# Sixteen weight splits made ahead move from the dilated heads to the convolution

## The chip, the cores and the metric

One core of a Trainium2 chip runs the whole program. The metric is the device time of one execution in microseconds: the median of several runs.

## The reference

Two transformer blocks run behind one another on one sequence of 1024 positions and 1024 channels, in float32. The first block has two layers, a gated short convolution and a dilated attention with 8 heads; the second an attention over selected keys and a gated feed-forward with a convolution. Cut to what matters here:

```python
mod = silu(c) @ w_mod + b_mod                      # per layer: shift, scale, gate
h, gate = rms_norm(x, g) * (1 + scale) + shift, gate
# layer 0
b_gate, c_gate, xin, z = split(h @ conv_w_in, 4)
x = x + gate * ((b_gate * conv3(c_gate * xin) * silu(z)) @ conv_w_out)
# layer 1: per head 3 groups (rates 1, 4, 16) of q and k, one v, one z
q, k, v, z = split(h @ dil_w_in, ...)              # q, k rotated
o = softmax-weighted sum over the groups of banded_attention(q_g, k_g, v)
x = x + gate * ((o * silu(z)) @ dil_w_out)
# second block: a_w_in, a_w_qi, a_w_uq, a_w_uk, a_w_uv, a_w_o, then f_w_in, f_w_out
```

## The kernel before

**Products.** A float32 product is made of three TensorE matmuls, high times high, high times low and low times high; every operand is kept as a rounded part `hi` and a rest `lo`. All of them are recorded at line 256. `gemm` multiplies one weight of 128 by 1024 with both halves of 512 positions: 24 matmuls for each half.

**Weights.** There are two ways to get one. `weight()` loads the raw weight on SyncE's queue (L376) into one of three slots `wraw`, ScalarE copies its high part (L377) and GpSimd subtracts (L378) into one of three pairs `wring`. `ready()` does this ahead, for the weights of the second block (`w2i` to `w3i`, 64 steps): a load (L353) into a slot of the same ring `wraw`, a copy by ScalarE into the one page `bench` (L354), a subtraction by VectorE in place (L355), and two stores to memory of the chip, of the high part (L357) and of the low part (L358). Later `weight()` loads such a pair in one go. Each step is started by `later.go()`. A slot of `wraw` is free again when the subtraction (L378), or the second store (L358), has read it.

**Order.** SyncE issues all these loads and stores in one queue, in a fixed order: an L357 waits for ScalarE, an L358 for VectorE, and an L353 or L376 for its slot, and what stands behind waits too. Each engine works in a fixed order as well. A scheduler sets these orders at build time; it simulates the engines and moves instructions of independent work past one another, so the order is not that of the code.

**The convolution** (L648 to L661) runs over columns j of 128 channels. A column has four weights `w0i` (`conv_cx`, `conv_zb`), whose products go to banks of PSUM in turn. VectorE reads them, at L561 (c times x) and L572 (b times z), and so frees the banks; `conv_out` makes the convolution and the gate. Beside it `modvec` makes the vectors of later layers: each `modblock` loads 512 KB of `wmod` (L298) into a page in turn, VectorE multiplies and sums it (L301) and adds the bias (L303). Some `w1v` weights of the next layer are loaded there too (L699). SyncE's names for the pages of `wmod` are `page_829` to `page_831`.

**The heads** (L945 to L981). For each of 8 heads six blocks of q and k are made, three groups of each, a block z, and then `attend`, whose scores go to PSUM (128x256 products) and are taken out by VectorE: L771 takes the maximum of two rows of blocks of the first group, in two pairs of instructions, one for each bank; L775 follows; L790 does it for the other groups. Between them L978 makes the gate from z, in two halves. In the code before, a split ahead is started after each of the six blocks, after z, and after `attend`: 8 in a head, 64 in all.

The function is long; the program prints here what the change touches.

Of the kernel before, what the change touches and what calls it, by code (L numbers as in the profile page):

```python
# [200 lines left out]
def emit(tc, I, OUT):  # L201
# [14 lines left out]
    with sp as sp, pp as pp, dp as dp:  # L216
# [34 lines left out]
        ar = Arena(pages, page_tile)  # L251
# [135 lines left out]
        def gemm(w, h, chunks, m=128, tag="mm"):  # L387

            whi, wlo = w
            out = {c: psum(tag) for c in chunks}  # L390
            kn = whi.shape[1]
            for c in chunks:
                for k in range(kn):
                    hi, lo = h[k][c]
                    mm(out[c][:m], whi[:, k], hi.r, k == 0, False)
                    mm(out[c][:m], whi[:, k], lo.r, False, False)
                    mm(out[c][:m], wlo[:, k], hi.r, False, k == kn - 1)
            return out
# [76 lines left out]
        def free_h(H, c):  # L475
            for k in range(len(H)):
                for b in H[k][c]:
                    b.free()
                H[k][c] = None
# [84 lines left out]
        def conv_zb(j, chunks, sz, ws=None, pz=None, pb=None):  # L564
            wz, wb = ws or (weight(I["w0i"][24 + j]), None)
            pz = pz or gemm(wz, H, chunks)
            for c in chunks:
                sz[c] = ar.new(512)
                A.activation(sz[c].f, pz[c], AF.Silu)
            pb = pb or gemm(wb or weight(I["w0i"][j]), H, chunks, tag="po")  # L570
            for c in chunks:
                V.tensor_mul(sz[c].f, sz[c].f, pb[c])  # L572

        def conv_out(j, t, sz):
            for c in range(2):
                u = ar.new(512)
                tv = lambda d: t.f[:, 512 * c + d:512 * c + d + 512]
                kc = lambda d: ck[d][:, j:j + 1]
                A.activation(u.f, tv(1), AF.Copy, scale=kc(1))
                V.scalar_tensor_tensor(u.f, tv(0), kc(0), u.f, op0=OP.mult, op1=OP.add)  # L580
                V.scalar_tensor_tensor(u.f, tv(2), kc(2), u.f, op0=OP.mult, op1=OP.add)
                V.tensor_mul(u.f, u.f, sz[c].f)
                Y[j][c] = new2()
                split(*Y[j][c], u.f, engine=G)
                u.free()
                sz[c].free()
            t.free()
# [56 lines left out]
            b.free()  # L644
        mring.extend(ar.new(1024) for _ in range(3))
        conv_out(0, *ts[0])
        pending = [2, 3, 4, 5, 6, 7, 8, 9, 10, 11]
        for j in range(1, 8):  # L648
            t, sz = ts[1] if j == 1 else new_t()
            if j > 1:  # L650
                conv_cx(j, (0, 1), t)
                conv_zb(j, (0, 1), sz)
            if j == 7:
                free_h(H, 0)
                free_h(H, 1)
            conv_out(j, t, sz)
            for _ in range(2 if j in (1, 3, 5) else 1):
                modvec(pending.pop(0))

        def weight_own(src, bufs):  # L660
# [4 lines left out]
            raw.free()  # L665
            bufs.extend((hi, lo))
            return tuple(b.r.rearrange("p (k m) -> p k m", k=8) for b in (hi, lo))

        bench = []
        later = Steps(ready(["w2i", "w2k", "w2q", "w2uk", "w2uv", "w2uq", "w2o", "w3i"]))  # L670

        def outproj(win, Y, c, gate, xold, xnew, each, apart=()):

# [271 lines left out]
        for h in range(HEADS):  # L945
# [5 lines left out]
            for g in range(3):  # L951
                for t, off, pad in ((q, 0, 0), (k, 24, 64)):
                    p = block(off + 8 * g + h)
                    later.go()
                    for c in range(2):
                        if g == 0:
                            at = lambda v: v[:, pad + 512 * c:pad + 512 * c + 512]
                        else:
                            at = lambda v: v.rearrange("p (j n) -> p n j",
                                                       j=8)[:, 64 * c:64 * c + 64]  # L960
# [7 lines left out]
                for b, part in zip(vs[-1], vd):  # L968
                    dma(b.f.rearrange("p (t n) -> p t n", n=128), src(part))
            p = block(56 + h)  # L970
            later.go()
            if h == HEADS - 1:
                free_h(H, 0)
                free_h(H, 1)
# [3 lines left out]
                V.scalar_tensor_tensor(sz.f[:, CH(c)], sz.f[:, CH(c)], 1.0, p[c], op0=OP.add,  # L978
                                       op1=OP.mult)
            attend(h, q, k, vs, sz)  # L980
            later.go()  # L981
        later.finish()
        for b in rope + mask1:
            b.free()
# [686 lines left out]
```

## Time and profile before

| | |
|---|---|
| median of 3 runs | 2758.61 us (2758.21 to 2761.03) |
| the profiled execution | 2767.96 us, span 2766.2 us, mean granted clock 0.974 |
| TensorE (PE) busy | 2610.6 us, 94% |
| VectorE (DVE) busy | 1535.2 us, 55% |
| ScalarE (ACT) busy | 1123.5 us, 41% |
| GpSimd (POOL) busy | 1001.8 us, 36% |
| L355, the splits' subtraction | 64 of them, 85.9 us |
| L354, the splits' copy | 64 of them, 67.4 us |

The convolution ends near 416 us, the heads run from about 600 to 1400 us, the second block from there to the end. TensorE's share is high in all stages, so an engine's busy time tells little; the idle time of TensorE, the wait that ends it, and the granted clock, which is 1.0 at 2.4 GHz, tell where time lies. Idle time of another engine matters only where TensorE stands behind it.

### The profile page before, as it was taken

What the parts mean: (1) busy time and instruction counts of PE and PEld (TensorE: products, weight loads), DVE (VectorE), ACT (ScalarE), POOL (GpSimd) and SP (SyncE); (2) the same over time, 40 slices, a digit from 0 to 9 for tenths busy, and PEclk for the clock granted to TensorE, in tenths of its full rate; (3) what the DMA queues carried; (4) which work ended last, traced back from release to release, by engine and by line L of the source; (5) the groups of instructions that cost most, each with busy time, mean ns of one, the idle gap of its engine ahead of it and who ended that gap; (6) DMA issues with size and microseconds to landing.
All of it is one profiled execution on the core that took longest, in us unless ns stands there. A gap on an engine that the chain in (4) does not pass through costs nothing. (4 is left out here: it accounts for less than half of the span.)

```text
span 2766.2 us, 34054 instructions
## 1 busy us (share of the span) xinstructions
PE 2610.6 (94%) x12070; PEld 2150.3 (78%) x12070; DVE 1535.2 (55%) x3260; ACT 1123.5 (41%) x1938; POOL 1001.8 (36%) x770
## 2 busy tenths in 40 slices
PE   8998999899999999999989888899999989999998
PEld 7886888788877878878867666678788767878887
DVE  7697222324666666666676699899655540222211
ACT  4211223324545545545443657674444432111132
POOL 1132327415535535535546334212211165200053
PEclk9999999999999999999999989999999999999999
DMA  7476214566365465456445573686666763667632
GB/s 291 162 273 234 88 66 158 163 202 220 131 229 198 140 220 206 141 203 214 157 140 177 205 247 103 229 262 224 207 212 213 242 203 103 207 239 259 226 117 73
DMA packets 208582, 524.67 MB, mean 190 GB/s; under 512 B 22258, under 2 KB 82202, under 8 KB 192796
## 3 DMA queue, kind: packets, MB, share of 16 engines
q1 hardware_dynamic: 199052, 497.20, 52.4%
q0 software_dynamic: 9216, 25.17, 3.1%
q8 instruction: 95, 1.56, 0.2%
q14 instruction: 75, 0.61, 0.1%
q10 hardware_dynamic: 144, 0.14, 0.0%
HBM read 394.03 MB, written 129.97 MB: 189 GB/s over the span
## 5 line engine op out<-in xcount | busy, mean ns | idle before, releaser
L256 PE MATMUL p<-page,wring 128*128 128x512 f32 (+2 forms) x8586 | 2023.9, 393 | 62.7 <-ACT page L384 11.4
L256 PEld LDWEIGHTS p<-page,wring 128*128 128x128 f32 (+1 forms) x8586 | 1605.9, 190 | 411.4 <-issue 20.2
L256 PE MATMUL p<-page,page 128*128 128x512 f32 (+5 forms) x2811 | 592.4, 354 | 75.3 <-DVE page L771 11.6
L378 POOL TENSOR_TENSOR wring<-wraw,wring 128x1024 fp32r<-128x1024 f32 (+1 forms) x159 | 392.6, 2471 | 599.2 <-ACT wring L377 532.5
L256 PEld LDWEIGHTS p<-page,page 128*128 128x128 f32 (+1 forms) x2811 | 470.5, 201 | 165.5 <-issue 18.1
L377 ACT ACTIVATE wring<-wraw 128x1024 fp32r<-128x1024 f32 (+1 forms) x159 | 164.4, 1035 | 317.6 <-PE p L256 285.2
L385 POOL TENSOR_TENSOR page<-page,page 128x512 fp32r<-128x512 f32 (+1 forms) x87 | 132.2, 1528 | 397.4 <-ACT page L384 390.9
L384 ACT ACTIVATE page<-page 128x512 fp32r<-128x512 f32 (+1 forms) x136 | 87.1, 652 | 227.5 <-DMA page<-d 104.1
L735 POOL TENSOR_TENSOR page<-page,page 128x512 f32<-128x512 f32 x96 | 123.8, 1296 | 87.8 <-ACT page L734 87.8
L355 DVE TENSOR_TENSOR wraw<-wraw,page 128x1024 fp32r<-128x1024 f32 (+1 forms) x64 | 85.9, 1342 | 92.1 <-ACT page L354 82.5
L301 DVE SCALAR_TENSOR_TENSOR page<-page,page 128x1024 f32<-128x1024 f32 x88 | 116.4, 1323 | 34.3 <-DMA page<-wmod 34.1
L1543 DVE SCALAR_TENSOR_TENSOR page<-p,page,page 128x512 f32<-128x512 f32 (+1 forms) x17 | 12.2, 719 | 204.1 <-PE p L256 204.1
L354 ACT ACTIVATE page<-wraw 128x1024 fp32r<-128x1024 f32 (+1 forms) x64 | 67.4, 1054 | 142.3 <-DMA wraw<-w3i 73.4
L744 POOL TENSOR_TENSOR page<-page,page 128x512 fp32r<-128x512 f32 x64 | 95.7, 1496 | 60.3 <-ACT page L743 60.2
L742 DVE TENSOR_TENSOR page<-page 128x512 f32<-128x512 f32 x64 | 98.0, 1532 | 27.8 <-POOL page L735 27.8
L737 DVE TENSOR_TENSOR page<-p,page 128x512 f32<-128x512 f32 x96 | 66.0, 687 | 66.4 <-ACT page L734 62.0
L1267 ACT ACTIVATE page<-page,page 128x1024 bf16<-128x1024 f32 (+1 forms) x93 | 86.7, 933 | 35.4 <-DVE page L1290 31.1
L743 ACT ACTIVATE page<-page 128x512 fp32r<-128x512 f32 x64 | 57.1, 892 | 84.5 <-DVE page L742 84.2
L1377 POOL TENSOR_TENSOR page<-page,page 128x256 f32<-128x256 f32 x64 | 46.7, 737 | 107.5 <-DVE page L1397 51.5
L441 POOL TENSOR_TENSOR page<-page,page 128x512 f32<-128x512 f32 x39 | 52.2, 1338 | 85.2 <-ACT page L440 85.1
L683 DVE SCALAR_TENSOR_TENSOR page<-p,page,page 128x512 f32<-128x512 f32 x48 | 35.9, 748 | 84.2 <-PE p L256 84.1
L1270 DVE TENSOR_SCALAR_CACHE_REDUCE page<-page,page 128x768 bf16<-128x768 f32 (+1 forms) x93 | 81.5, 876 | 1.5
(214 smaller groups left out, 2303.4 us busy)
## 6 DMA issues: line engine op xcount, KB each, us to landing
wring<-d SPq DMA_DIRECT2D x122, 1024.0 KB, 5.8
d<-page SPq DMA_DIRECT2D x95, 512.0 KB, 3.8
page<-wmod SPq DMA_DIRECT2D x88, 512.0 KB, 4.5
d<-page SPq DMA_DIRECT2D x153, 256.0 KB, 4.0
d<-wraw SPq DMA_DIRECT2D x63, 512.0 KB, 3.5
page<-d SPq DMA_DIRECT2D x121, 256.0 KB, 3.2
wraw<-w1i SPq DMA_DIRECT2D x56, 512.0 KB, 3.5
wraw<-w3i SPq DMA_DIRECT2D x44, 512.0 KB, 3.3
```

The costliest lines, as they stand in the source:

```text
L256: lastn["mm"] = T.matmul(out, lhsT=l, rhs=r, start=start, stop=stop)
L301: V.scalar_tensor_tensor(w.f, w.f, 1.0, sil[j // 6].f, op0=OP.mult, op1=OP.mult, accum_out=m)
L355: V.tensor_sub(raw.r[:, :n], raw.f[:, :n], hi.f[:, :n])
L377: A.activation(hi.r[:, :n], raw.f[:, :n], AF.Copy)
L378: (lo_engine or G).tensor_sub(lo.r[:, :n], raw.f[:, :n], hi.f[:, :n])
L384: A.activation(hi.r[:, :n], src, AF.Copy)
L385: (engine or V).tensor_sub(lo.r[:, :n], src, hi.f[:, :n])
L735: G.tensor_mul(sw.f, sw.f, rope[1].f[:, CH(c)])
L742: V.tensor_tensor(a.f, a.f, sw.f, op=OP.add)
L744: G.tensor_sub(out[1], shape(a.f), out[2])
L1267: A.activation(junk.b[:, 0:sc.n], sc.f, AF.Sign, scale=-1.0, bias=at, accum_out=one)
L1270: V.tensor_scalar(junk.b[:, 0:sc.n], sc.f, at, None, op0=OP.is_ge, op1=OP.add, accum_out=one)
```

## The change

The two calls of `later.go()` after z and after `attend` are taken out of the head, so a head starts six splits and the eight heads 48. The generator and `bench` are made before the convolution. For columns 4 to 7 `later.go(4)` starts four splits in each, between `conv_zb` and `conv_out`, with a page for `bench` that is taken at column 4 and given back at column 7. The 64 steps keep their order, so in the convolution the 16 are `w2i` (4), `w2k`, `w2q`, `w2uk`, `w2uv`, `w2uq` (2 each of the last three) and four of `w2o`. Lines after 659 have moved by 3 and after 970 by 2 or 1 (L771 is now L774, L775 L778, L790 L793, L978 L980).

```diff
@@ -644,13 +644,19 @@
         conv_out(0, *ts[0])
+        bench = []
+        later = Steps(ready(["w2i", "w2k", "w2q", "w2uk", "w2uv", "w2uq", "w2o", "w3i"]))
         pending = [2, 3, 4, 5, 6, 7, 8, 9, 10, 11]
         for j in range(1, 8):
             t, sz = ts[1] if j == 1 else new_t()
             if j > 1:
                 conv_cx(j, (0, 1), t)
                 conv_zb(j, (0, 1), sz)
+            if j == 4:
+                bench.append(ar.new(1024))
+            later.go(4 if j > 3 else 0)
             if j == 7:
+                bench.pop().free()
                 free_h(H, 0)
                 free_h(H, 1)
             conv_out(j, t, sz)
...
-        bench = []
-        later = Steps(ready(["w2i", "w2k", "w2q", "w2uk", "w2uv", "w2uq", "w2o", "w3i"]))
...
             p = block(56 + h)
-            later.go()
...
             attend(h, q, k, vs, sz)
-            later.go()
         later.finish()
```

How this moves instructions is seen at three places. The first is SyncE's queue in the convolution, from the last raw weight of column 4 on. Before:

```order
L376 DMA wraw<-w0i 128x1024
L699 DMA page_831<-w1v 128x1024
L298 DMA page_829<-wmod 128x1024
L298 DMA page_830<-wmod 128x1024
L298 DMA page_829<-wmod 128x1024
L298 DMA page_830<-wmod 128x1024
L376 DMA wraw<-w0i 128x1024
L298 DMA page_829<-wmod 128x1024
L298 DMA page_830<-wmod 128x1024
```

and in the changed kernel:

```order
L376 DMA wraw<-w0i 128x1024
L298 DMA page_829<-wmod 128x1024
L298 DMA page_830<-wmod 128x1024
L298 DMA page_829<-wmod 128x1024
L298 DMA page_830<-wmod 128x1024
L298 DMA page_829<-wmod 128x1024
L353 DMA wraw<-w2i 128x1024
L298 DMA page_830<-wmod 128x1024
L298 DMA page_829<-wmod 128x1024
L357 DMA d_1677<-page_1130 128x1024
L358 DMA d_1677<-wraw 128x1024
L298 DMA page_830<-wmod 128x1024
```

The `w1v` load has moved behind, and between the `wmod` loads stand the load and the two stores of the first split; the next raw `w0i` comes at row 126 of the queue instead of 111.

The second place is VectorE at the products of column 4 (L561, which empties two banks), among the products of `wmod` (L301). Before:

```order
L561 TENSOR_TENSOR page_440<-page_832,p_1510 128x512
L301 SCALAR_TENSOR_TENSOR page_830,page_65<-page_830,page_88 128x1024
L580 SCALAR_TENSOR_TENSOR page_1130<-page_440,page_65,page_1130 128x512
L303 TENSOR_TENSOR page_65<-page_65 128x1
L591 MEMSET page_440 128x1
L301 SCALAR_TENSOR_TENSOR page_829,page_65<-page_829,page_88 128x1024
L303 TENSOR_TENSOR page_65<-page_65 128x1
L301 SCALAR_TENSOR_TENSOR page_830,page_65<-page_830,page_88 128x1024
L561 TENSOR_TENSOR page_440<-page_84,p_1511 128x512
```

and in the changed kernel:

```order
L355 TENSOR_TENSOR wraw<-wraw,page_1130 128x1024
L301 SCALAR_TENSOR_TENSOR page_830,page_65<-page_830,page_88 128x1024
L301 SCALAR_TENSOR_TENSOR page_829,page_65<-page_829,page_88 128x1024
L303 TENSOR_TENSOR page_65<-page_65 128x1 x2
L561 TENSOR_TENSOR page_440<-page_832,p_1510 128x512
L301 SCALAR_TENSOR_TENSOR page_830,page_65<-page_830,page_88 128x1024
L301 SCALAR_TENSOR_TENSOR page_829,page_65<-page_829,page_88 128x1024
L580 SCALAR_TENSOR_TENSOR page_1072<-page_440,page_65,page_1072 128x512
L303 TENSOR_TENSOR page_65<-page_65 128x1 x2
L325 SCALAR_TENSOR_TENSOR page_65<-page_65 128x8
L355 TENSOR_TENSOR wraw<-wraw,page_1130 128x1024
L561 TENSOR_TENSOR page_440<-page_84,p_1511 128x512
```

Two splits' subtractions (L355) have come in around the first L561. Counted from the load of `w0i` above, the first L561 stood behind 13 products of `wmod` and the second behind 16; now it is 11 and 13, with two and three L355 ahead of them.

The third place is VectorE at the end of a head, where the gate (L978, now L980), the scores' maxima (L771, now L774, printed as ISA) and a split meet. Before:

```order
L978 SCALAR_TENSOR_TENSOR page_5947<-page_5947,p_6527 128x512
L771 ISA page_5138,page_65<-p_6587,page_2645 128x256
L771 ISA page_65 128x1
L771 ISA page_5138,page_65<-p_6587,page_2645 128x256
L771 ISA page_65 128x1
L355 TENSOR_TENSOR wraw<-wraw,page_3641 128x1024
L771 ISA page_5138,page_65<-p_6599,page_2645 128x256
L771 ISA page_65 128x1
L771 ISA page_5138,page_65<-p_6599,page_2645 128x256
L771 ISA page_65 128x1
L775 TENSOR_SCALAR page_65<-page_65 128x2
L790 ISA page_4157,page_65<-p_6651,page_2713 128x384
```

and in the changed kernel:

```order
L980 SCALAR_TENSOR_TENSOR page_5214<-page_5214,p_5788 128x512
L355 TENSOR_TENSOR wraw<-wraw,page_3735 128x1024
L774 ISA page_4417,page_4247<-p_5842,page_2740 128x256
L774 ISA page_4247 128x1
L774 ISA page_4417,page_4247<-p_5842,page_2740 128x256
L774 ISA page_4247 128x1
L774 ISA page_4417,page_4247<-p_5854,page_2740 128x256
L774 ISA page_4247 128x1
L774 ISA page_4417,page_4247<-p_5854,page_2740 128x256
L774 ISA page_4247 128x1
L778 TENSOR_SCALAR page_4247<-page_4247 128x2
L980 SCALAR_TENSOR_TENSOR page_5214<-page_5214,p_5789 128x512
```

The split that stood between the two pairs of L771 stands ahead of both pairs of L774 now. (Each pair is two instructions, with a read of the accumulated maximum behind each.)

## Rows read from the trace of the kernel before

**Rows 1.** The windows of 100 us, one of them inside the heads: for each engine the busy time and the count of instructions, then the granted clock of TensorE as a share, the busy share of the DMA engines and their GB/s.

```profile
1000.00:1100.00 100.00, 95.31 (x474) 80.00 (x473) 64.28 (x121) 49.13 (x85) 48.74 (x37) 0.98 0.53 185
```

**Rows 2.** Who TensorE waited for in the eight heads, 620 to 1400 us: us in total, times, longest us.

```profile
PE p L256 <- DVE page L771: 11.6, 7, 3.0
PE p L256 <- DVE page L790: 8.1, 9, 1.2
PE p L256 <- DVE page L737: 7.1, 7, 1.0
```

**Rows 3.** The timeline of TensorE at the end of one head, 872 to 895 us: start, length, line, operation and count; in brackets the idle time before and what ended it. Products with `wring` are block products, those of 128x256 the scores and what follows them.

```profile
871.74 10.36 PE L256 MATMUL p<-page,wring 128*128 128x512 f32 x45
...
886.95 0.74 PE L256 MATMUL p<-page,page 128*128 128x256 f32 x5
887.45 1.64 PE L256 MATMUL p<-page,wring 128*128 128x512 f32 x6
891.74 0.84 PE L256 MATMUL p<-page,page 128*128 128x256 f32 x5 [2.66 <-DVE page L771]
893.76 1.65 PE L256 MATMUL p<-page,page 128*128 128x256 f32 x6 [1.18 <-DVE page L790]
```

**Rows 4.** The timeline of VectorE at the same place.

```profile
882.93 0.69 DVE L978 SCALAR_TENSOR_TENSOR page<-page,p 128x512 f32<-128x512 f32 x1 [2.40 <-ACT page L977]
883.54 0.42 DVE L771 CUSTOM_DVE_ANT_0 page<-p,page 128x256 f32<-128x256 f32 x1
...
884.23 0.08 DVE L771 DVE_READ_ACCUMULATOR2_ANT page<- 128x1 f32 x1
889.77 1.23 DVE L355 TENSOR_TENSOR wraw<-wraw,page 128x1024 fp32r<-128x1024 f32 x1 [5.47 <-ACT page L354]
...
891.60 1.64 DVE L775 TENSOR_SCALAR page<-page 128x2 f32<-128x2 f32 x1
893.15 0.54 DVE L790 CUSTOM_DVE_ANT_0 page<-p,page 128x384 f32<-128x384 f32 x1
```

**Rows 5.** The timeline of ScalarE there: a copy of a raw weight (L377) and one of a split ahead (L354).

```profile
881.36 1.06 ACT L377 ACTIVATE wring<-wraw 128x1024 fp32r<-128x1024 f32 x1 [3.16 <-DMA wraw<-w1i]
...
888.63 1.06 ACT L354 ACTIVATE page<-wraw 128x1024 fp32r<-128x1024 f32 x1 [5.73 <-DMA wraw<-w3i]
```

**Rows 6.** The timeline of GpSimd there: the subtraction that makes the low part of a weight.

```profile
882.50 2.40 POOL L378 TENSOR_TENSOR wring<-wraw,wring 128x1024 fp32r<-128x1024 f32 x1 [5.58 <-PE p L256]
```

**Rows 7.** The timeline of SyncE's queue there: a raw weight (L376), a split's load (L353) and its second store (L358).

```profile
873.41 0.42 SPq L376 DMA_DIRECT2D wraw<-w1i  x1
...
884.92 0.33 SPq L353 DMA_DIRECT2D wraw<-w3i  x1
...
891.03 0.33 SPq L358 DMA_DIRECT2D d<-wraw  x1
```

**Rows 8.** The group of the splits' subtraction L355 in 600 to 1400 us: count, busy time, mean ns, and VectorE's idle time before it by releaser.

```profile
L355 DVE TENSOR_TENSOR wraw<-wraw,page 128x1024 fp32r<-128x1024 f32 (+1 forms) x61 | 82.2, 1348 | 87.8 <-ACT page L354 78.1 <-POOL page L842 6.1 <-DMA wraw<-w1i 2.7
```

**Rows 9.** Windows of 5 us behind the waits of that head, with the columns of the first group.

```profile
890.00:895.00 5.00, 2.08 (x11) 1.87 (x12) 5.00 (x16) 2.31 (x7) 2.50 (x1) 0.89 0.68 246
895.00:900.00 5.00, 5.00 (x25) 4.48 (x25) 3.48 (x15) 4.93 (x15) 1.96 (x4) 0.77 0.53 210
```

**Rows 10.** Windows of 20 us in the convolution, with the same columns.

```profile
210.00:230.00 20.00, 14.69 (x53) 11.64 (x52) 17.43 (x35) 2.88 (x4) 2.71 (x1) 0.83 0.81 285
230.00:250.00 20.00, 16.12 (x70) 12.69 (x69) 15.09 (x22) 4.07 (x5) 6.86 (x3) 1.00 0.58 199
250.00:270.00 20.00, 18.13 (x77) 14.75 (x78) 13.22 (x24) 4.17 (x6) 4.88 (x2) 0.98 0.74 255
270.00:290.00 20.00, 17.05 (x62) 13.39 (x62) 16.81 (x26) 4.79 (x8) 7.30 (x4) 0.85 0.53 192
290.00:310.00 20.00, 20.00 (x90) 16.57 (x89) 3.47 (x5) 4.54 (x6) 6.52 (x4) 1.00 0.17 54
```

**Rows 11.** Who TensorE waited for in 190 to 300 us: us in total, times, longest us.

```profile
PE p L256 <- DVE page L303: 7.4, 2, 5.3
PE p L256 <- DVE page L561: 4.8, 2, 2.9
PE p L256 <- DVE page L572: 2.6, 2, 1.8
```

**Rows 12.** Who VectorE waited for there.

```profile
DVE page L301 <- DMA page<-wmod: 17.0, 16, 2.8
```

**Rows 13.** The timeline of SyncE's queue in the convolution: five loads of wmod, and one raw weight.

```profile
238.23 13.96 SPq L298 DMA_DIRECT2D page<-wmod  x5
252.28 0.38 SPq L376 DMA_DIRECT2D wraw<-w0i  x1
```

**Rows 14.** The timeline of ScalarE there: the copy of that weight.

```profile
279.84 1.05 ACT L377 ACTIVATE wring<-wraw 128x1024 fp32r<-128x1024 f32 x1
```

**Rows 15.** Who TensorE waited for behind the heads, 1400 to 2766 us.

```profile
PE p L256 <- DVE page L1183: 13.4, 5, 8.1
...
PE p L256 <- DVE page L1276: 4.9, 1, 4.9
```

**Rows 16.** A window of 20 us there, with the columns of the first group.

```profile
1580.00:1600.00 20.00, 7.58 (x17) 5.51 (x18) 19.50 (x54) 16.03 (x32) 16.21 (x12) 0.58 0.66 236
```

## The prediction

> **What bounds the kernel now.** TensorE is busy in 94% of the span, so only the places where it stands idle, or runs at the lower clock, can give time back. I read the windows first, then who PE waits for, then the timelines of one head. In a hundred microseconds of the heads PE is busy for 95, at a granted clock of 0.98 [rows 1]. The table of waits names who ends it: in the eight heads PE waits 11.6 us for L771, which empties the score banks of the attention, 8.1 us for L790 behind it and 7.1 us for L737 [rows 2]. No line of the splits is in that table. The timelines show them a step further back.
>
> In the head of 800 to 903 us PE ends its last block products at 889.09, stands 2.66 us until L771 has emptied the second pair of banks, does five matmuls and stands again 1.18 us for L790 [rows 3]. VectorE had emptied the first pair by 884.3 and was then idle for 5.47 us, not because the second pair's scores were missing (PE had issued them at 886.95), but because a split's subtraction, L355, stands in its order between the two pairs, and that waited for ScalarE's copy L354 [rows 3, 4]. The copy at 888.63 had waited 5.73 us for the split's load [rows 5]. The load left SyncE only at 884.92, which is when GpSimd ended the subtraction L378 of 882.50 to 884.90 that held the load's slot in the raw ring [rows 6, 7]. That subtraction began 0.08 us after the copy L377 of 881.36 had ended (its row names PE as the last releaser), and the copy had waited for a weight load that SyncE had issued at 873.41, 8 us before [rows 5 to 7]. So a chain of a raw load, its split into hi and lo, and a split ahead behind it holds an engine that PE needs.
>
> **The heads: what goes and what stays.** Two of eight splits leave each head, 16 in all. Each costs VectorE 1.35 us [rows 8], a copy on ScalarE of 1.06 us [rows 5], and three transfers of 512 KB. None of this is a term by itself: VectorE is busy 64 us in the hundred [rows 1]. What counts is where a remaining split stands. The order of the changed kernel still has one at this place: behind the first L980 (L978 before) and ahead of both pairs of L774 (L771 before). So the two pairs are no longer parted, but both now hang on that split's load.
>
> When does that load leave? Its slot is again that of the raw weight three loads before, whose copy must first be made. That weight is now fetched ahead of two of the value loads, in a pair of issues, so it isn't late any more; what its copy waits for is a place in the ring of finished weights, which PE frees when the last q/k block ends. PE's run of 45 matmuls from 871.74 is 21 of that block and 24 of the next, so the place is free at about 871.74 + 21/45 x 10.36 = 876.6 [rows 3]. Copy 1.06 us, subtraction 2.4 us, with 0.2 us between: the load leaves at about 880.3 instead of 884.92. In the trace, load issue to the end of L355 took from 884.92 to 891.00, 6.1 us [rows 4, 7]; so L355 would end at 886.4, the first pair at 887.15 and the second at 887.9 (0.76 us a pair). PE wants the first pair at 886.95 and the second about 1 us later: waits of 0.2 us and none. Then the two-column L775 (1.64 us), the second L980 (0.69 us as L978) and the first L790 (0.54 us) follow on VectorE, to 890.8; PE comes there at 888.7. So PE still stands 0.2 + 2.1 = 2.3 us instead of 3.84 us: 1.5 us saved a head. The wait changes its name from L774 to L793.
>
> The clock adds to this. After the stall the granted clock is 0.89 in one 5 us stretch and 0.77 in the next, a part of it spent at 1.2 instead of 2.4 GHz [rows 9]; 5 x 0.11 + 5 x 0.23 = 1.7 us are lost so. I give back a share of it as large as that of the wait, 1.5/3.84 x 1.7 = 0.7 us. Together 2.2 us a head, in seven heads **-15 us**. The bounds: all of the two waits and of the clock loss, 11.6 + 8.1 + 7 x 1.7 = -32 us; and a loss, if the load is late (first rival). I stay near the middle since the load's time rests on two engines' orders. The waits for L737 are a second place, earlier in the head (one of 1.0 us each, [rows 2]); I put nothing down for them.
>
> **The convolution: columns 5 to 7.** From 290 us on PE is full, VectorE has 3.47 us of work in 20, ScalarE 4.54, and the DMA engines a share of 0.17 [rows 10]. Twelve splits in three columns of 44 us (4 weights x 48 matmuls, at 10.36 us for 45 [rows 3]) need 16 us of VectorE, 13 us of ScalarE and 36 transfers. At 512 KB and 285 GB/s, the highest rate of these windows [rows 10], 36 are 66 us in 132. All that lies beside PE: 0. It would cost something if a weight's slot in the raw ring came too late; but the load that left at 252.28 was copied at 279.84 only, 27 us later [rows 13, 14], while a split has its slot for 6.1 us from the load to the issue of its second store [rows 7] and the time that this takes to land.
>
> **The convolution: column 4.** Its four splits land at 225 to 290 us, where things are tight. PE waits 7.4 us for L303, 4.8 us for L561 and 2.6 us for L572 in 190 to 300 us [rows 11]: VectorE takes the wmod products of L301 in order, waits 17.0 us in all for their loads, and the L561 and L572 that empty PE's banks stand among them [rows 12]. With the change, a w1v load and part of these products move behind: the first L561 of column 4 stands after 11 of the 18 products instead of 13, the second after 13 instead of 16, but with two and three splits' L355 ahead of them. Five products of about 2.8 us (five wmod issues took 13.96 us [rows 13]) come later, three L355 at 1.35 us come in: for the second L561, 3 x 2.8 - 3 x 1.35 = 4.3 us earlier, if the loads come as fast as before. But the 4 splits bring 12 transfers of 1.84 us, 22 us, into the same queue. The DMA engines have 0.42, 0.26 and 0.47 of three 20 us windows free there, 23 us [rows 10]. It just goes in, if it falls in the gaps. I take **-2 us**; the bounds are -9 us (all of the 14.8 us of [rows 11] but the longest wait for L303, 5.3 us, which stands before the splits) and +22 us (none of the transfers falls in a gap). I stay near the small end because the products are held by the landing of each load with two pages in turn, not by the engines' rate.
>
> **Behind the heads** nothing is changed by name, but the scheduler deals the order anew: in the first search of the block after, the search steps start some rows earlier among the norm's products, and the L1184 (L1183) move by a few rows up and down. PE waits 13.4 us there for L1183 and 4.9 us for L1276, and from 1580 to 1600 us it is busy for 7.58 us at a clock of 0.58 [rows 15, 16]. I see no reason for a sign: 0, with 12 us (what PE lacks in that window) to either side.
>
> **The sum.** The profiled execution took 2767.96 us, 9.35 us more than the median of 2758.61 us. 2767.96 - 15 - 2 + 0 = 2750.96 us; less the 9.35 us, **2741.6 us**.
>
> **Rivals.** First, slower: the split before L774 is late. It decides by one point. If its load leaves as in the trace, at 884.92, L355 ends at 891.0, the first pair is out at 891.76, and PE stands 4.8 us there and 2 us more for L793, 6.8 us instead of 3.84; 3 us a head, 21 us in seven, 2758.6 + 21 - 2 = 2778 us. The wait of before is reached when L355 ends at 888.0, so when the load leaves at about 882. For it: the margin against my 880.3 is 1.6 us, and a weight load took 8 us in this place. Against it: fewer transfers are in flight, and the weight is fetched earlier. Chance 0.13.
>
> Second: the wait changes its name and nothing more. The load leaves near 882, PE stands as long as before: only the -2 us, 2757 us. Chance 0.18.
>
> Third, slower or even: column 4. The wmod loads wait behind the splits' transfers, VectorE takes its order late, L572 and L561 release PE's banks late: +22 us and with the -15 us of the heads 2766 us. The page "DMA: Bandwidth & Descriptors" of the Trainium skill, section "Queues, rings and completion order", speaks for it: each DMA engine consumes the descriptors of a ring in order, and SyncE has one ring on each, so a wmod load stands behind what a split queued; at its limit of 358 GB/s the 12 transfers would be an estimated 18 us. No row here shows which it is. Against it stands the free share of 23 us. Chance 0.11.
>
> Fourth: all of the heads' waits at L774 and L793 go, with the clock: 2758.6 - 32 - 2 = 2725 us. Chance 0.10. The forecast keeps 0.48.
>
> **How the numbers follow.** The forecast's own range is 2741.6 with 12 us to each side for what lies behind the heads. To hold 8 in 10 the range takes in the fourth (2725, and a few us below) and the second and third (2757, 2766): 2720 to 2768; the first stays out. About 0.2%, 5.5 us, is what a measurement of this kernel can tell from no change. Faster by more than that (under 2753): the fourth, nearly all of the forecast, a little of the second: 0.59. Within it: most of the second, a part of the third and of the forecast's upper end: 0.20. Slower: the first, part of the third: 0.21.
>
> **What would show it.** Right: PE's waits for L774 under 3 us over the heads, those for L793 about 10 us or more; windows of the heads with PE busy about 97 us in a hundred; the split's load leaving about 6 us before VectorE's first L774; PE full from 290 to 415 us as before. Wrong: waits for L774 of 4 us a head (first), PE's waits for L303, L561 and L572 in 225 to 310 us above 15 us (third), or a window behind 1560 us that lost or gained more than 12 us.

## The result, and the profile after

The changed kernel takes 2715.91 us (median of 4 runs, 2710.75 to 2724.10), the kernel before 2759.82 us beside it: a ratio of 0.9831, 95% interval 0.9804 to 0.9857. It is 44 us faster, where 17 were forecast, and lies 4 us under the range.

The profiled execution took 2724.1 us with a span of 2722.3 us. It is cut here in three stages at one matmul that each head does once, the transpose L804: from the start to that of the first head, the seven periods to that of the last, and what lies behind. The rows give the first and last start in a trace (one of the eight stands in a row of its own). Of the kernel before:

```profile
L804 PE MATMUL p<-page x7: 271/271/272, 697.8 to 1400.2; 128*16 128x128 f32 x7
```

and of the changed one, where the line is L807:

```profile
L807 PE MATMUL p<-page x7: 271/271/272, 698.4 to 1377.5; 128*16 128x128 f32 x7
```

| stage, us | before | changed | difference | forecast |
|---|---|---|---|---|
| to the first head's mark | 697.8 | 698.4 | +0.6 | -2 |
| seven head periods | 702.4 | 679.1 | -23.3 | -15 |
| behind the last mark | 1366.0 | 1344.8 | -21.2 | 0 |

So the front came out as forecast, the heads gave half as much again, and half of the gain came from a stretch in which nothing is changed by name. The two profiled executions of the changed kernel that were made later gave 697.4, 675.9, 1346.4 and 692.3, 675.2, 1345.1 us: a stage repeats within 2 to 6 us, and in runs below whose heads have one order on VectorE the heads lie up to 7 us apart. Of the kernel before there is one trace only.

**The heads.** The waits of TensorE from 620 to 1380 us, where L774, L793, L860 and L740 answer to L771, L790, L857 and L737 of [rows 2] (columns as there):

```profile
PE p L256 <- DVE page L860: 10.8, 6, 4.4
PE p L256 <- DVE page L740: 7.1, 7, 1.0
PE p L256 <- DVE page L793: 1.1, 1, 1.1
```

The wait for the maxima is gone altogether, that for L793 nearly. L740 is as before. L860, the end of the attention, has risen: the same view of before has 4.1 us for L857. The timeline of TensorE at the place of [rows 3], in the head that ends at 894 us:

```profile
879.25 2.40 PE L256 MATMUL p<-page,page 128*128 128x256 f32 x19
881.41 3.02 PE L256 MATMUL p<-page,wring 128*128 128x512 f32 x12
884.26 0.74 PE L256 MATMUL p<-page,page 128*128 128x256 f32 x5
```

The scores of both pairs are among the products from 879.25 on; those of 884.26 belong to the other groups, and the bank that they take is the one that the first pair frees. TensorE runs through this place without a break. VectorE there, answering to [rows 4]:

```profile
877.92 1.22 DVE L355 TENSOR_TENSOR wraw<-wraw,page 128x1024 fp32r<-128x1024 f32 x1 [2.59 <-ACT page L354]
879.80 0.42 DVE L774 CUSTOM_DVE_ANT_0 page<-p,page 128x256 f32<-128x256 f32 x1 [0.66 <-PE p L256]
...
880.52 0.42 DVE L774 CUSTOM_DVE_ANT_0 page<-p,page 128x256 f32<-128x256 f32 x1
...
881.21 1.57 DVE L778 TENSOR_SCALAR page<-page 128x2 f32<-128x2 f32 x1
```

The split's L355 still stands ahead of both pairs, but it is over at 879.14, and VectorE then waits 0.66 us for TensorE's scores, not the other way round. The reason is on SyncE's queue, answering to [rows 7], and on GpSimd, answering to [rows 6]:

```profile
871.90 0.33 SPq L353 DMA_DIRECT2D wraw<-w3i  x1
```

```profile
869.48 2.40 POOL L378 TENSOR_TENSOR wring<-wraw,wring 128x1024 fp32r<-128x1024 f32 x1 [3.18 <-ACT wring L377]
```

The split's load left at 871.90, at the end of the L378 of 869.48, and 12.4 us before the products of 884.26; before it left 2.0 us before the same products, at 886.95 [rows 3, 7]. The windows with the columns of [rows 1, 9] show PE at the full clock through the place that had 0.89 and 0.77:

```profile
800.00:900.00 100.00, 96.82 (x493) 81.51 (x492) 61.88 (x129) 49.58 (x89) 53.39 (x40) 1.00 0.46 159
885.00:890.00 5.00, 5.00 (x33) 4.49 (x33) 3.49 (x11) 3.52 (x10) 1.91 (x4) 1.00 0.36 147
890.00:895.00 5.00, 5.00 (x27) 4.12 (x26) 1.86 (x11) 2.51 (x8) 2.24 (x5) 1.00 0.57 216
```

**The convolution.** TensorE's waits from 190 to 300 us, answering to [rows 11], and the windows of [rows 10]:

```profile
PE p L256 <- DVE page L572: 10.2, 3, 4.2
PE p L256 <- DVE page L561: 1.9, 1, 1.9
PE p L256 <- DVE page L303: 0.9, 1, 0.9
```

```profile
230.00:250.00 20.00, 18.02 (x74) 14.42 (x73) 12.95 (x29) 1.47 (x2) 3.54 (x2) 0.91 0.72 237
250.00:270.00 20.00, 15.82 (x58) 12.49 (x57) 17.27 (x23) 4.67 (x7) 9.21 (x4) 0.83 0.75 286
270.00:290.00 20.00, 20.00 (x90) 16.58 (x89) 14.67 (x25) 5.60 (x7) 2.40 (x1) 1.00 0.89 312
290.00:310.00 20.00, 20.00 (x90) 16.56 (x89) 8.42 (x12) 5.28 (x7) 7.41 (x4) 1.00 0.76 276
```

13.0 us of waits instead of 14.8, with the name changed to L572, while the DMA share from 230 to 290 us, 0.58, 0.74 and 0.53 before [rows 10], is 0.72, 0.75 and 0.89. From 290 us on PE is full as before, though VectorE is busy for 8.42 us instead of 3.47 and the DMA share is 0.76 instead of 0.17.

**Behind the heads.** Two of TensorE's waits there, answering to [rows 15]:

```profile
PE p L256 <- DVE page L1277: 16.1, 1, 16.1
...
PE p L256 <- DVE page L1184: 3.6, 4, 2.2
```

The waits for L1184 fell from 13.4 to 3.6 us, one wait of 16.1 us for L1277 took the place of 4.9 us. The two don't add up to the 21 us. More is seen in the group of the searches' update, first and last start of 120 (L1290 before, L1291 after):

```profile
L1290 DVE SCALAR_TENSOR_TENSOR page<-page x120: 146/158/1307, 1569.7 to 1906.6; 128x1 int32<-128x1 int32 x60, 128x2 int32<-128x2 int32 x60
```

```profile
L1291 DVE SCALAR_TENSOR_TENSOR page<-page x120: 143/158/1248, 1546.2 to 1868.4; 128x1 int32<-128x1 int32 x60, 128x2 int32<-128x2 int32 x60
```

The searches ran over 336.9 us before and over 322.2 us now: 14.7 of the 21 us. A window of 100 us among them, before and changed, with the columns of [rows 1]:

```profile
1600.00:1700.00 100.00, 84.88 (x390) 66.00 (x390) 91.89 (x314) 61.12 (x149) 36.61 (x52) 0.95 0.59 185
```

```profile
1580.00:1680.00 100.00, 87.14 (x421) 67.06 (x419) 94.35 (x325) 66.72 (x163) 42.15 (x60) 1.00 0.63 190
```

VectorE, the third number, is busier there than PE, the first, in both, so that its order may well set the pace here; no run tests this reading alone.

### The profile page after: what moved, and what is told of

Its sections match the earlier page's. It is cut to its first block, busy times and chain, and to the rows that moved or that the text cites. A ratio compares the mean times of both kernels' runs of the same rounds, so it can differ in the third digit from the quotient of the medians.

```text
span 2722.3 us, 34072 instructions
## 1 busy us (share of the span) xinstructions
PE 2588.6 (95%) x12070; PEld 2136.3 (78%) x12070; DVE 1528.9 (56%) x3260; ACT 1128.4 (41%) x1940; POOL 1009.8 (37%) x770
## 5 line engine op out<-in xcount | busy, mean ns | idle before, releaser
L256 PE MATMUL p<-page,wring 128*128 128x512 f32 (+2 forms) x8586 | 2017.9, 393 | 42.2 <-DVE page L572 11.5
L256 PE MATMUL p<-page,page 128*128 128x512 f32 (+5 forms) x2816 | 578.2, 349 | 64.9 <-DVE page L860 12.6
L378 POOL TENSOR_TENSOR wring<-wraw,wring 128x1024 fp32r<-128x1024 f32 (+1 forms) x159 | 387.9, 2440 | 551.6 <-ACT wring L377 479.6
L256 PEld LDWEIGHTS p<-page,page 128*128 128x128 f32 (+1 forms) x2816 | 461.8, 197 | 151.4 <-issue 18.4
L377 ACT ACTIVATE wring<-wraw 128x1024 fp32r<-128x1024 f32 (+1 forms) x159 | 164.6, 1036 | 301.0 <-PE p L256 272.7
L355 DVE TENSOR_TENSOR wraw<-wraw,page 128x1024 fp32r<-128x1024 f32 (+1 forms) x64 | 78.8, 1231 | 126.4 <-ACT page L354 122.2
L301 DVE SCALAR_TENSOR_TENSOR page<-page,page 128x1024 f32<-128x1024 f32 x88 | 126.2, 1436 | 40.2 <-DMA page<-wmod 39.9
L747 POOL TENSOR_TENSOR page<-page,page 128x512 fp32r<-128x512 f32 x64 | 103.7, 1622 | 61.8 <-ACT page L746 61.6
L354 ACT ACTIVATE page<-wraw 128x1024 fp32r<-128x1024 f32 (+1 forms) x64 | 67.4, 1053 | 142.8 <-DMA wraw<-w3i 40.9
L1544 DVE SCALAR_TENSOR_TENSOR page<-p,page,page 128x512 f32<-128x512 f32 (+1 forms) x17 | 12.2, 719 | 202.9 <-PE p L256 202.9
L740 DVE TENSOR_TENSOR page<-p,page 128x512 f32<-128x512 f32 x96 | 66.1, 689 | 78.5 <-ACT page L737 73.1
L745 DVE TENSOR_TENSOR page<-page 128x512 f32<-128x512 f32 x64 | 95.4, 1492 | 25.6 <-POOL page L738 25.6
L736 ACT ACTIVATE page<-p 64x512 f32<-64x512 f32 x96 | 57.3, 596 | 72.4 <-PE p L256 54.1
L1511 ACT ACTIVATE page<-p 128x512 f32<-128x512 f32 x44 | 26.2, 596 | 142.2 <-PE p L256 142.2
```

The costliest lines, as they stand in the source:

```text
L256: lastn["mm"] = T.matmul(out, lhsT=l, rhs=r, start=start, stop=stop)
L301: V.scalar_tensor_tensor(w.f, w.f, 1.0, sil[j // 6].f, op0=OP.mult, op1=OP.mult, accum_out=m)
L354: A.activation(hi.r[:, :n], raw.f[:, :n], AF.Copy)
L355: V.tensor_sub(raw.r[:, :n], raw.f[:, :n], hi.f[:, :n])
L377: A.activation(hi.r[:, :n], raw.f[:, :n], AF.Copy)
L378: (lo_engine or G).tensor_sub(lo.r[:, :n], raw.f[:, :n], hi.f[:, :n])
```

## The experiments

The names: "place" is the theory that a split costs what its load is late by if it stands on VectorE between TensorE's scores and the end of the attention; its rival "number" is that each split that leaves the heads gives a share. For the stretch behind the heads, the theory is that its order alone was dealt anew; the rival, that it follows from what the heads leave. Stages are those of the table above, in us.

| run | ratio to before | 95% | front | heads | behind |
|---|---|---|---|---|---|
| the change, again | 0.9830 | 0.9798 to 0.9861 | 697.4 | 675.9 | 1346.4 |
| the change, third time | 0.9824 | 0.9803 to 0.9845 | 692.3 | 675.2 | 1345.1 |
| seven a head | 0.9935 | 0.9912 to 0.9958 | 698.4 | 703.9 | 1347.3 |
| eight a head, early | 0.9888 | 0.9861 to 0.9914 | 694.9 | 667.5 | 1371.6 |
| pages dealt anew behind the heads | 0.9866 | 0.9840 to 0.9892 | 696.8 | 679.0 | 1353.0 |
| columns 5 to 7 only | 0.9880 | 0.9848 to 0.9911 | 704.0 | 672.4 | 1349.3 |
| six a head, early | 0.9924 | 0.9907 to 0.9942 | 694.4 | 699.7 | 1347.4 |
| convolution part only | 0.9894 | 0.9876 to 0.9913 | 695.9 | 690.3 | 1345.1 |
| a spare page in the kernel before | 0.9933 | 0.9910 to 0.9957 | 701.6 | 709.2 | 1341.7 |
| eight early and the spare page | 0.9795 | 0.9776 to 0.9814 | 695.3 | 665.3 | 1346.9 |

### The change twice more

No edit. The first stands beside the three runs from six a head to the spare page, the second beside the last run, each on the chip of those runs.

> The changed kernel once more, beside the next three on one chip. Heads 679 us for seven periods, 1345 us behind them, total 0.983 of the kernel before; within 4 us in each stage.

> The changed kernel beside it on the same chip: 0.983 of the kernel before, stages 698, 677 and 1346 us.

Both came out in the ratio as the change did in the result; the front of the third time lay 6 us lower than in the result.

### Seven a head

```diff
-            later.go(4 if j > 3 else 0)
+            later.go(2 if j > 3 else 0)
...
             attend(h, q, k, vs, sz)
+            later.go()
```

> Only the split after z leaves each head (seven a head stay), eight splits go to columns 4 to 7, two in each. VectorE's order at the end of a head is that of the change: one split behind the first half of the gate and ahead of all scores' maxima. Theory (place: what counts is that no split whose load is late stands among the maxima): no wait of TensorE for the maxima (L774-type), seven head periods together 679 to 684 us as with the change, total 2712 to 2724. Rival (number: every split that leaves the heads gives its share, through fewer transfers and less work on ScalarE and VectorE): half of the heads' gain, periods about 690 us, total about 2727. The order behind the heads is that of the change, so 1345 us are expected there.

(The edit keeps the split after the attention and drops the one after z.) The order behind the heads did what was expected, 1347.3 us. The heads fell out of both expectations: 703.9 us, as long as before, and with them the total, 2749.68 us. The wait for the maxima is indeed not in the table of waits, but this is:

```profile
PE p L256 <- DVE page L860: 22.3, 6, 4.5
```

VectorE, and then GpSimd, at the stall of 4.50 us that ends at 920.77 in one head:

```profile
896.71 1.23 DVE L355 TENSOR_TENSOR wraw<-wraw,page 128x1024 fp32r<-128x1024 f32 x1 [2.23 <-ACT page L354]
...
914.71 1.23 DVE L355 TENSOR_TENSOR wraw<-wraw,page 128x1024 fp32r<-128x1024 f32 x1
915.85 4.27 DVE L841 TENSOR_SCALAR page<-page,page 128x256 f32<-128x256 f32 x8
920.04 1.87 DVE L860 TENSOR_TENSOR page<-p,page 128x512 fp32r<-128x512 f32 x3
```

```profile
917.15 2.55 POOL L378 TENSOR_TENSOR wring<-wraw,wring 128x1024 fp32r<-128x1024 f32 x1 [11.54 <-ACT wring L377]
```

Two splits stand later in the same chain: one among the maxima of the other groups at 896.71, 2.23 us late by its copy, and one at 914.71, just ahead of the scaling L841 and of L860, on which TensorE waits. So the theory as tested here, for the maxima alone, was too narrow: the chain from the scores to L860 is one. But the splits are not all of it. Four of the six waits are 4.3 to 4.5 us long, and in just these four heads the eight L841 took 4.27 us, because one of them ended only with a subtraction of GpSimd, as here (917.15 to 919.70). In the other two, with the split at the same place, the waits were 2.2 and 2.5 us and the scaling took half as long:

```profile
1323.78 2.19 DVE L841 TENSOR_SCALAR page<-page,page 128x256 f32<-128x256 f32 x8
```

So some 8 of the 22.3 us (four times 2.1) came with GpSimd. How much of the rest each of the two splits costs is not shown: the next run has splits in this chain too, and hardly a wait for its end. The rival's half of the gain isn't there either.

### Eight a head, early

The kernel before, with

```diff
                     p = block(off + 8 * g + h)
-                    later.go()
+                    later.go(2 if g == 0 else 1)
...
             p = block(56 + h)
-            later.go()
...
             attend(h, q, k, vs, sz)
-            later.go()
```

> The kernel before with its eight splits a head, none in the convolution; the two of a head that were started after z and after the attention are started with the first two blocks instead. No split stands between the gate and the maxima any more. Theory (place): TensorE's wait for the maxima, 11.6 us before, under 3 us, seven periods 679 to 690 us instead of 702. Rival (number): 702 us, since as many splits and transfers stay. Behind the heads the order is dealt anew, so the total is read only with the stages apart.

```profile
PE p L256 <- DVE page L790: 1.3, 2, 1.1
PE p L256 <- DVE page L857: 1.0, 2, 0.7
```

The wait for the maxima is gone. Eight splits a head, and the seven periods are 667.5 us, 12 less than with the change and less than the 679 to 690 expected. Number falls. VectorE in one head (L771 are the maxima; the last split ahead of them ends at 866.84, seven us before the first pair, and the second pair waits for TensorE):

```profile
865.62 1.22 DVE L355 TENSOR_TENSOR wraw<-wraw,page 128x1024 fp32r<-128x1024 f32 x1 [2.08 <-ACT page L354]
...
873.73 0.43 DVE L771 CUSTOM_DVE_ANT_0 page<-p,page 128x256 f32<-128x256 f32 x1
...
876.14 0.42 DVE L771 CUSTOM_DVE_ANT_0 page<-p,page 128x256 f32<-128x256 f32 x1 [0.96 <-PE p L256]
...
884.43 1.23 DVE L355 TENSOR_TENSOR wraw<-wraw,page 128x1024 fp32r<-128x1024 f32 x1 [1.20 <-ACT page L354]
...
902.12 1.22 DVE L355 TENSOR_TENSOR wraw<-wraw,page 128x1024 fp32r<-128x1024 f32 x1
```

The last two rows are splits in the chain behind the maxima, one of them 1.20 us late, the other behind the scaling and just ahead of L857. TensorE waits 1.0 us in all for L857, so a split in this chain can be free.

Behind the heads it is as slow as before, 1371.6 us.

### Pages dealt anew behind the heads

The changed kernel, with

```diff
         bench[0].free()
+        ar.new(1024).free()
```

> The changed kernel, and a page taken and given back at once behind the heads: no instruction more, but the pages and so the order behind the heads are dealt anew; convolution and heads stand in the same order as with the change. Theory (the 21 us that the stretch behind the heads lost come from its order, which the change dealt anew by chance): heads 679 us as with the change, the stretch behind them other than 1345 us by 5 to 25 us, total 2716 to 2740. Rival (they come from the state in which the heads leave the engines and queues): 1345 us within 3, total 2716.

Heads 679.0 us, as with the change; behind them 1353.0 us, 8.2 us more than the first time and 6.6 and 7.9 us more than the two others, and those three lie within 1.6 us. No instruction was added. The rival's 1345 within 3 fell.

### Columns 5 to 7 only

```diff
-            if j == 4:
+            if j == 5:
                 bench.append(ar.new(1024))
-            later.go(4 if j > 3 else 0)
+            later.go((0, 0, 0, 0, 0, 6, 5, 5)[j])
```

> The changed kernel with its sixteen splits in columns 5 to 7 (6, 5 and 5) and none in column 4. Theory (column 4 cost and gave next to nothing, the splits are hidden): the time from the start to the first head's end within 4 us of the change, total 2712 to 2720. Rival (the splits of column 4 cost TensorE the waits for L572, which rose from 2.6 to 11.5 us): 6 to 10 us less, total about 2708.

The front is not shorter but longer, 704.0 us, 5.6 us more than the first time, and the total, 2729.86 us, is above both expectations. From 190 to 300 us TensorE waits 12.1 us here (7.3 for L572, 4.8 for L303) against 13.0 with the change, so the splits of column 4 cost next to nothing that could be had back. A part of what is longer lies in the columns that took more; TensorE's waits from 300 to 500 us, where the change has none:

```profile
PE p L256 <- ACT wring L377: 2.1, 1, 2.1
PE p L256 <- POOL wring L378: 1.4, 1, 1.4
```

With six splits in a column some of the raw weights' own copies and subtractions come late, 3.5 us in all; four a column show no such wait. The rest of the difference is not explained.

### Six a head, early

The changed kernel, with `later.go((2, 1, 0)[g])` after each of the six blocks.

> The changed kernel with its sixteen splits in the convolution and six a head, but started early in the head: two with each of the first two blocks, one with each of the next two, none with the last two. Theory (place: a split costs what its load is late by, when it stands on VectorE between the scores and the end of the attention): waits of TensorE for L774, L793 and L860 together under 4 us, seven periods 660 to 668 us (679 with the change), order behind the heads that of the change, 1345 us, total about 14 us under the change. Rival (number): six a head in either, so 679 us.

Both expectations failed: 699.7 us instead of 660 to 668 or 679, and 2743.15 us in total, 22 more than the change beside it. Started early in the code doesn't mean early on the engines. The scheduler left a split behind the first half of the gate, as in the change, and here its load was late:

```profile
PE p L256 <- DVE page L774: 10.8, 6, 2.2
PE p L256 <- DVE page L860: 9.4, 6, 2.1
```

With L793 the waits are 23.8 us where under 4 were expected. SyncE's load, ScalarE's copy and VectorE's subtraction of that split:

```profile
980.02 0.42 SPq L353 DMA_DIRECT2D wraw<-w3i  x1
```

```profile
986.28 1.06 ACT L354 ACTIVATE page<-wraw 128x1024 fp32r<-128x1024 f32 x1 [6.17 <-DMA wraw<-w3i]
```

```profile
987.37 1.23 DVE L355 TENSOR_TENSOR wraw<-wraw,page 128x1024 fp32r<-128x1024 f32 x1 [4.96 <-ACT page L354]
```

The load left at 980.02, 7.2 us before TensorE came, at 987.19, to the products that want the first pair's bank, in place of the 12.4 us of lead that it has in the change, and VectorE stood 4.96 us for it. Six a head in either, 24 us apart: this, too, is place against number.

### Convolution part only

The changed kernel with the two `later.go()` of the head put back, so that eight a head are done and the last two heads have none.

> The sixteen splits in the convolution as in the change, but eight a head started as before, so that the 48 left are done in six heads and the last two have none. In those six VectorE has a split between the two pairs of maxima again. Theory (place): the wait for the maxima returns in the heads with splits, 1.5 to 3 us each, and their periods are about 101 us; the periods without splits about 96 us; seven periods 695 to 700 us. Rival (what leaves the heads for the convolution is what counts): same sum of work in the heads as in the change, 679 us.

The distances of the eight marks: 105.8, 99.9, 102.3, 102.6, 95.7, 95.4, 88.6 us, with 8, 8, 8, 8, 4, 0 and 0 of L355 in them. The heads with eight splits are as long as before, those with none 95.4 (the last period is a shorter one in all kernels), and TensorE waits for L774 again, 9.5 us in five times. The sum of 690.3 us misses the theory's 695 to 700 by 5 and the rival's 679 by 11. In the run of eight early the distances are 95.5, 95.7, 95.4, 97.3, 95.7, 95.4, 92.5 with 8 of L355 in each of the first six and 2 in the last. So eight well-placed splits a head cost next to nothing: 95.4 to 95.7 us in five of six periods, 97.3 in one, against 95.4 without any. The room in the convolution isn't what the heads gained by.

### A spare page in the kernel before

The kernel before, with a page held at columns 4 to 7 and not used:

```diff
+            if j == 4:
+                spare = ar.new(1024)
             if j == 7:
+                spare.free()
                 free_h(H, 0)
```

> The kernel before, and a page taken at column 4 and given back at column 7 with nothing in it: no instruction more and no split moved. Convolution and heads stand in the order of before, behind them the order is dealt anew by the pages. Theory (the stretch behind the heads moves with its order alone): heads 702 us as before; behind them other than 1366 us by more than 5 us, down to 1345 or up to 1380. Rival (that stretch follows what the heads leave): 1366 us within 4, total as before.

Behind the heads 1341.7 us, 24 less than before, with all splits where they were. The heads are not shorter, 709.2 us: 7 us more than before with VectorE's order in them unchanged, so that far apart can two traces of one order lie. The searches' update, L1293 here:

```profile
L1293 DVE SCALAR_TENSOR_TENSOR page<-page x120: 144/158/1245, 1581.8 to 1903.2; 128x1 int32<-128x1 int32 x60, 128x2 int32<-128x2 int32 x60
```

321.4 us, as with the change. The rival's 1366 within 4 fell.

### Eight early and the spare page

The two edits above in one: the kernel before, no split moved to the convolution.

> The kernel before with no split moved to the convolution: eight a head, two each with the first two blocks as in the run with eight early, and the spare page of columns 4 to 7. Heads in the order of the run with eight early, behind them word for word the order of the change. Theory (two causes and no third: no late split among the maxima, and the order behind the heads): 695 us to the first head's end, 667 us for seven periods, 1345 us behind, total 2704 to 2714, so as fast as the change or a little faster. Rival (the room in the convolution is needed for the gain): 2720 or more.

```profile
PE p L256 <- DVE page L794: 1.4, 2, 1.1
...
PE p L256 <- DVE page L861: 0.4, 1, 0.4
```

The stages came as expected: 695.3, 665.3 and 1346.9 us. 0.9795, 0.9776 to 0.9814, and beside it the change at 0.9824: as fast as the change or a little faster (2708.63 us against 2714.22 on one chip), with nothing moved out of the heads. It is the fastest version found.

## Why the prediction was wrong

**The step that failed: "Behind the heads", 0 with 12 us to either side.** It measured -21.2 us, and by that the sum left the range: without them the time would be 2737 us. I saw that the order was dealt anew and took the idle time of one window for the bound. But in the searches VectorE is busier than TensorE (91.89 against 84.88 in the window above), so TensorE's free time was no bound for what another order of VectorE's instructions can give; it showed as 14.7 us in the searches' length. A spare page without any split moved gave 24 us twice: 1366.0 to 1341.7 in the kernel before, 1371.6 to 1346.9 with eight early. All seven runs whose last 1656 instructions on VectorE stand one by one in the order of the change lie at 1345 to 1349 us (the change three times, seven a head, columns 5 to 7, six early, eight early with the spare page); those with other orders are spread from 1342 to 1372. The searches took 336.9 us before and 335.6 with eight early, and 321 to 325 in the ten other traces. What in an order makes them shorter isn't settled. The counts of the search that VectorE makes itself (L1270, L1271 after) start ahead of the norm's products (L448) with the change and among them before; but with the pages dealt anew they start among them too (L1272 at 1559.3, L448 from 1555.1 to 1564.1 us) and the searches took 325.1 us, so that this place alone is not the cause.

**The heads: right in mechanism, mis-sized.** -23.3 us against -15. That L355 between the pairs held TensorE, and that it would stand ahead of both now, is as the trace shows. The term that was mis-sized is the load's lead. The prediction has "the load leaves at about 880.3", 6.65 us before the products at 886.95 that want the first pair's bank. It left 12.4 us before the same products. The condition was right: the raw weight's copy waited for the end of the last q/k block. Its time was misread. The 45 products of [rows 3] that end at 882.10 are not half of that block and half of the next, they are all of the block z, since ScalarE reads the last q/k block's products (L733) for the last time at 874.26. The rows are that one, of before, and the copy of the changed kernel:

```profile
874.26 0.60 ACT L733 ACTIVATE page<-p 64x512 f32<-64x512 f32 x1
```

```profile
868.34 1.06 ACT L377 ACTIVATE wring<-wraw 128x1024 fp32r<-128x1024 f32 x1 [1.65 <-PE p L256]
```

The 48 products of z take 11.05 us at 10.36/45 each, so the q/k block of before ended near 871.05 and not at 876.6. With the copy, the subtraction and the 0.2 us of the prediction the load could leave at 874.7, an estimate, 12.2 us before 886.95.

Besides, line by line:

- "PE had issued them at 886.95". The scores of the second pair are among the products from 881.94 on, as VectorE's second pair at 880.52, ahead of 884.26, shows in the changed kernel. That the split held them stands all the same.
- "The wait changes its name from L774 to L793", 2.3 us a head. It went: 1.1 us in eight heads. The bound of -32 us held.
- The loss of clock came back whole in the head shown: 0.89 and 0.77 became 1.00.
- "The waits for L737 are a second place", for which I put nothing: 7.1 us, unchanged. Not seen: L860, the end of the same chain, rose by 6.7 us. At the longest of these waits, 4.40 us, the scaling L841 ahead took 4.26 us, and 2.19 in the other heads of that trace, since one of its instructions ended only with a subtraction of GpSimd (909.93 to 912.38); what the other waits rose by is not explained. In seven a head L860 came to 22.3 us, 11.5 more than with the change, and the heads' gain was gone.

**The convolution: right, as far as can be told.** -2 forecast, +0.6 measured, with a stage that repeats within 6 us. Waits of 13.0 instead of 14.8 us; "columns 5 to 7: 0" held with four a column; with six there were 3.5 us of waits.

**The rivals.** The first, a late split ahead of L774, is not what the change does, but it is what its neighbour does: with six a head started early the heads are 700 us. My point of decision, the load's lead, was the right quantity. The second fell. The third fell: the DMA share rose to 0.72 to 0.89 and TensorE's waits did not. What the page "DMA: Bandwidth & Descriptors" of the Trainium skill states on rings was not what bound here. The fourth had the mechanism: the waits for L774 and L793 fell from 19.7 us to 1.1, and the clock came back. Its 32 us were too many, since L860 took 6.7 us back; the heads' 23.3 lie between them and the forecast's 15.

**What can't be told from the two traces alone.** Read by its description, the change worked by taking sixteen splits out of the heads. It didn't: no split has to leave them. It worked by two side effects of new orders, each of which can be had without it, and each of which a nearby version loses. That dealing pages and order anew does it is shown by the runs; whether behind the heads it is the order alone, and which instruction in it, is not.

## What to carry to other kernels

When an engine works in a fixed order, ask of each side task not how long it is but what it waits for and who stands behind it; eight side tasks a head were free in one order, while in another six, one of them late by up to 5 us, cost (699.7 - 675.9)/7 = 3.4 us a head. If a scheduler or an allocator deals the order, a change moves stages that it doesn't name: put the spread of those stages (here some 30 us in 1350) into the range, and before believing a gain, measure it stage by stage beside a version in which the order is dealt anew with nothing moved.

## What the hardware showed

VectorE's L775 (2 columns, 0.16 us at 894.70 in the same head) took 1.64 us in the row of [rows 4], from 891.60 to 893.24; GpSimd's subtraction of a weight there:

```profile
890.71 2.50 POOL L378 TENSOR_TENSOR wring<-wraw,wring 128x1024 fp32r<-128x1024 f32 x1 [5.82 <-ACT wring L377]
```

It ended at 893.21. In the changed kernel L778 ran from 881.21 to 882.78, and GpSimd had

```profile
880.36 2.40 POOL L378 TENSOR_TENSOR wring<-wraw,wring 128x1024 fp32r<-128x1024 f32 x1 [7.23 <-ACT wring L377]
```

to 882.76. In the runs of eight early and six early the same pair ended at 879.98 and 879.95, and at 990.85 and 990.82 us. In all twelve traces 190 of the 384 instructions of this line took more than 0.3 us, and every one of them ended 0.02 to 0.03 us after an instruction of GpSimd, as if it had been held for it. The scaling L841 was held in the same way in seven a head: 2.43 us for one instruction that takes 0.35 otherwise.

The page "GPSIMD Engine Reference" of the Trainium skill, section "8. Key points", says that GpSimd shares its SBUF interfaces with VectorE, and names as the case VectorE's instructions in a two-port mode or with two inputs from SBUF. The trace agrees with the sharing, at up to 1.5 us a time for L775 and 2.1 for L841, here on the chain that TensorE waits for; in which mode the two run is not seen. No run took it away.
